# Block inverses of the gated-delta stage: even and odd columns in separate partitions, two masks dropped

## The chip, the core and the metric

The kernel runs on one core of one Trainium2 chip. The metric is the device time of one execution in microseconds (us); the table below gives the median of three runs.

## What is computed

One step of a hybrid decoder: a half-step SwiGLU feed-forward, a mixer, a second feed-forward, with 1,024 prompt tokens and 8 sequences of 8 new tokens. The mixer has two branches that are added under sigmoid gates: sliding-window attention (over the prompt, and of the new tokens over a cache of keys and values), and a gated delta rule with 8 heads of 128. The change is in the gated delta rule, in the inverse of a unit lower triangular matrix per head and chunk:

```python
    A = jnp.where(strict, jnp.einsum('bhnid,bhnjd->bhnij', kb, kc) * decay, 0.0)
    eye = jnp.eye(C, dtype=f32)
    T = lax.linalg.triangular_solve(A + eye, jnp.broadcast_to(eye, A.shape), left_side=True, lower=True)
    u_val = jnp.einsum('bhnij,bhnjv->bhniv', T, vb)
    w_key = jnp.einsum('bhnij,bhnjd->bhnid', T, kb * jnp.exp(gc)[..., None])
```

Outputs are the new token states, the last convolution rows, the recurrent matrices, keys and values.

## The kernel before

The work runs in one long program: first feed-forward, gates and prompt attention of the mixer, attention of the new tokens (`att_sample`, L974 to L1041, called sample attention below), the gated delta stage (`gdn`, L1224), the second feed-forward. A scheduler sets the order of each engine's queue; every engine then works its queue strictly in that order. Buffers come from pools that are stacked in one memory: when a stage ends, the next stage's pools are laid over the same addresses, and a tile may be written once every tile that held its addresses before has been read for the last time.

**Dense work.** For each head, q, k and v come from matmuls of the normed input with weight slices (L250 to L252, three passes, result `psgh` in three banks of PSUM). `conv_dense` copies them into a tile `ext` (pool "e", three buffers; L1178 clears its head, ACT copies at L1179, L1184 and L1186), `conv_taps` (L1200 to L1210) makes the convolution and SiLU from it, the tile `yh`. The dense matmuls are also what the program puts between the steps of slow chains, so that PE has work.

**Sample attention.** SP loads both caches (L983, L984). PE transposes the keys (L995, tile `pst`), makes scores (L1011, L1012, tile `pss`); a softmax on DVE and ACT; PE transposes the weights (L1026, L1027) into the tile `ptS`; then eight groups of sixteen matmuls (L1033, L1034) into the one bank `pso`, each copied out by DVE (L1039, eight copies). L1040 on DVE gates the sum and SP writes it out (L1041).

**The inverse** (`stage_t`, L1337). Per head k·kᵀ (L1351) gives nine chunks of 128x128, scaled to `am0` (L1367). They are written to memory (`adr`, L1377) and the 36 diagonal blocks of 32x32 are read back, one block to a partition (tile `L`, L1378). X starts as the identity (L1379, L1380). 31 steps of two DVE instructions (L1384 a product, L1385 a sum) make X the inverse of each block; step l works on (31−l) x (l+1) elements of each partition. L1389 makes the transposed copy, L1391 writes both to memory (`tdr`), L1397 loads them as diagonal blocks of 128x128 (`t4`, two groups of four chunks, each straight and transposed). `levels` (L1406) then joins blocks of 32 to 64 and of 64 to 128 with small matmuls (L1416, L1426, L1427, L1440, L1445); its weights are `am`, which POOL makes from `am0` by a mask multiplication (L1410, L1437). Then the chain over the chunks of the head (L1456 and on) uses the result.

`stage_t`, the chain and the gated output of a head run as generators beside the dense work (class `Weave`): each yields the PE time of its step and a gap, and dense steps are put in until the gap is over.

Of the kernel before, what the change touches and what calls it, by code (L numbers as in the profile page):

```python
# [9 lines left out]
F32 = mybir.dt.float32  # L10
# [3 lines left out]
ALU = mybir.AluOpType  # L14
# [4 lines left out]
P = 128  # L19
# [8 lines left out]
NCH = 9  # L28
# [4 lines left out]
BLK = 32  # L33
# [19 lines left out]
def constants():  # L53
# [17 lines left out]
        "m2": (j // 64 == i // 64) & (j % 64 < 32) & (i % 64 >= 32),  # L71
        "m3": (j < 64) & (i >= 64),
# [83 lines left out]
class Core:  # L156
# [1068 lines left out]
    def gdn(self):  # L1225
        nc, v = self.nc, self.nc.vector
        with ExitStack() as st:
            gp = self.pool("gdn", stack=st)
            a, n = self.off["m2"]
            self.m2 = gp.tile([P, 2, 32], F32, name="m2")  # L1230
            nc.sync.dma_start(self.m2, self.i["c_pack"][:, a:a + n].rearrange("p (b u j) -> p b u j", b=2, u=2)[:, :, 1, :])
            a, n = self.off["m3"]
            self.m3 = gp.tile([P, 64], F32, name="m3")
            nc.sync.dma_start(self.m3, self.i["c_pack"][:, a + 64:a + n])
# [12 lines left out]
            bp = Pools(self, st, ("L", "X", "pr", "am"), ("S0", "kg", "vt", "qk"), ("t4",), ("R", "o1", "vn", "S", "jk", "*"), ("ot", "zg", "me", "s4"), ("e",), ("y",), ("dm", "am0"))  # L1247
# [77 lines left out]

    def decay(self, bp, h, d):
# [11 lines left out]
    def stage_t(self, bp, h, d, prev):  # L1338
# [36 lines left out]
        L, X = (bp.tile([nb, BLK, BLK], F32, tag=x, bufs=1, name=self.name(x)) for x in ("L", "X"))  # L1375
        pr = bp.tile([nb, BLK * BLK // 4], F32, tag="pr", bufs=1, name=self.name("pr"))
        nc.sync.dma_start(self.rows_view(ad, 0), am0)  # L1377
        nc.gpsimd.dma_start(L, self.diag_view(ad, 0))  # L1378
        nc.gpsimd.memset(X, 0.0)  # L1379
        nc.gpsimd.memset(X.rearrange("p a b -> p (a b)")[:, ::BLK + 1], 1.0)  # L1380
        for l in range(BLK - 1):
            n, m = BLK - 1 - l, l + 1
            tmp = pr[:, :n * m].rearrange("p (a b) -> p a b", b=m)
            v.tensor_tensor(out=tmp, in0=L[:, l, m:, None].broadcast_to([nb, n, m]), in1=X[:, l, None, :m].broadcast_to([nb, n, m]), op=ALU.mult)  # L1384
            v.tensor_tensor(out=X[:, m:, :m], in0=X[:, m:, :m], in1=tmp, op=ALU.add)  # L1385
            if l % 2:
                yield 0, X_STEP
                self.lab = f"h{h}"
        v.tensor_copy(L, X.rearrange("p i j -> p j i"))  # L1389
        for u, src in enumerate((X, L)):  # L1390
            nc.gpsimd.dma_start(self.diag_view(td, u), src)  # L1391
# [14 lines left out]
    def levels(self, bp, h, A, t4):  # L1406
        nc, v = self.nc, self.nc.vector
        self.lab = f"h{h}"
        am = bp.tile([P, 4, 2, 32], F32, tag="am", bufs=2, name=self.name("am"))
# [532 lines left out]
```

## Time and profile before

| | us |
|---|---|
| median of three runs (2808.99 to 2811.06) | 2810.89 |
| the profiled execution | 2810.84 |
| span in its trace | 2809.1 |
| granted clock of TensorE, mean | 0.983 |
| PE busy | 2691.2 (96%) |
| DVE busy | 1982.4 (71%) |
| ACT busy | 1237.3 (44%) |
| POOL busy | 563.7 (20%) |

Times in the trace count from the start of the span. Of it, the sample attention and the gated delta stage take 1183 to 1957. The clock is the share of full speed that TensorE was granted; 1.00 is 2.4 GHz and 0.50 is 1.2 GHz. A time in brackets behind an instruction is the idle time of its engine just before it, with the instruction that ended it.

### The profile page before, as it was taken

How to read it: one execution, taken by the hardware profiler on the slowest of the kernel's cores; microseconds unless marked ns; L12 is line 12 of the kernel's file. 1: busy time of each engine (PE TensorE's matmuls, PEld its weight loads, DVE VectorE, ACT ScalarE, POOL GpSimd, SP SyncE). 2: the span in 40 equal slices, each digit the busy share in tenths (PEclk: the TensorE clock that was granted, in tenths of full speed). 3: DMA queues.
4: the chain of work that ended last, by engine and by line, in shares of the span. 5: the costliest groups of instructions: out<-in, count | busy, mean ns of one | idle time of the engine just before them, and what ended most of it. 6: DMA issues, size and time to landing. Idle time of an engine off the chain costs nothing.

```text
span 2809.1 us, 50868 instructions
## 1 busy us (share of the span) xinstructions
PE 2691.2 (96%) x19887; PEld 2523.4 (90%) x19887; DVE 1982.4 (71%) x4502; ACT 1237.3 (44%) x2904; POOL 563.7 (20%) x585
## 2 busy tenths in 40 slices
PE   6999999999989999999999999999999999998998
PEld 6899999999978888887788888888989999997998
DVE  6777787564665777777887776785678878767545
ACT  5333322233334767753655455546444233223333
POOL 3222221231010000031332222221002212205110
PEclk9999999999999999999999999999999999999999
DMA  4243322546332333342333333334533322216562
GB/s 143 91 158 127 112 101 90 191 135 144 107 105 54 85 85 78 97 100 63 90 98 78 67 94 90 89 82 145 191 118 117 103 88 102 100 57 237 129 147 78
DMA packets 236871, 306.66 MB, mean 109 GB/s; under 512 B 14405, under 2 KB 184214, under 8 KB 236598
## 3 DMA queue, kind: packets, MB, share of 16 engines
q1 hardware_dynamic: 203252, 222.21, 25.9%
q0 software_dynamic: 33312, 81.19, 10.6%
q8 instruction: 156, 2.56, 0.4%
q14 instruction: 85, 0.70, 0.1%
q10 hardware_dynamic: 66, 0.02, 0.0%
HBM read 212.19 MB, written 84.19 MB: 106 GB/s over the span
## 4 chain that ended last, share of the span: by engine, by line
PE 77%; DVE 9%; DMA 5%; ACT 3%; issue 3%; POOL 1%; SPq 0%; DVEq 0%; ACTq 0%; POOLq 0%
PE pst L252 13%; PE pst L250 13%; PE pst L251 13%; PE pst L715 4%; PE pst L714 4%; PE pst L713 4%; PE psgh L250 3%; PE psgh L251 3%; PE psgh L252 3%; PE psg L250 3%; PE psg L252 3%; PE psg L251 3%; PE pso L943 1%; DMA adr<-am0h 1%; PE pst L936 1%
## 5 line engine op out<-in xcount | busy, mean ns | idle before, releaser
L251 PE MATMUL pst<-x,u 128*128 128x256 f32 (+3 forms) x2656 | 780.4, 294 | 1.0 <-DVE x L226 1.0
L250 PE MATMUL pst<-x,u 128*128 128x256 f32 (+3 forms) x2040 | 610.8, 300 | 12.1 <-ACT x L225 11.1
L252 PE MATMUL pst<-x,u 128*128 128x256 f32 (+3 forms) x2040 | 605.6, 297 | 0.0
L251 PEld LDWEIGHTS pst<-x,u 128*128 128x128 f32 x2656 | 503.8, 190 | 7.1 <-DVE x L226 1.5
L250 PEld LDWEIGHTS pst<-x,u 128*128 128x128 f32 x2040 | 386.3, 190 | 19.3 <-ACT x L225 12.6
L252 PEld LDWEIGHTS pst<-x,u 128*128 128x128 f32 x2040 | 387.4, 190 | 4.6
L225 ACT CAST u<-raw 128x512 fp32r<-128x512 f32 x308 | 186.4, 617 | 323.3 <-PE pst L252 300.6
L715 PE MATMUL pst<-x,u 128*128 128x272 f32 x1008 | 293.3, 292 | 13.8 <-DVE u L226 13.8
L252 PE MATMUL psgh<-xhl,wlh 128*128 128x512 f32 (+2 forms) x912 | 303.7, 333 | 0.0
L713 PE MATMUL pst<-x,u 128*128 128x272 f32 x1008 | 290.6, 292 | 7.4 <-ACT x L225 7.1
L714 PE MATMUL pst<-x,u 128*128 128x272 f32 x1008 | 293.2, 292 | 4.5 <-DVE x L226 4.5
L226 DVE TENSOR_TENSOR u<-raw,u 128x512 fp32r<-128x512 f32 x308 | 216.5, 712 | 49.6 <-ACT u L225 49.3
L334 DVE TENSOR_TENSOR tm<-pst,tm 128x256 f32<-128x256 f32 (+1 forms) x400 | 168.0, 434 | 103.0 <-PE pst L252 100.9
L252 PE MATMUL pst<-xhl,u 128*128 128x256 f32 (+2 forms) x808 | 237.8, 295 | 2.5 <-DVE u L226 2.5
L250 PE MATMUL pst<-xhl,u 128*128 128x256 f32 (+2 forms) x808 | 236.7, 294 | 2.2 <-ACT u L225 2.2
L715 PEld LDWEIGHTS pst<-x,u 128*128 128x128 f32 x1008 | 192.8, 191 | 14.6 <-DVE u L226 14.6
L713 PEld LDWEIGHTS pst<-x,u 128*128 128x128 f32 x1008 | 191.6, 192 | 8.3 <-ACT x L225 7.5
L714 PEld LDWEIGHTS pst<-x,u 128*128 128x128 f32 x1008 | 192.9, 191 | 4.9 <-DVE x L226 4.9
L252 PEld LDWEIGHTS psgh<-xhl,wlh 128*128 128x128 f32 x912 | 172.9, 190 | 12.2
L252 PEld LDWEIGHTS pst<-xhl,u 128*128 128x128 f32 x808 | 153.2, 190 | 5.9 <-DVE u L226 2.9
L250 PEld LDWEIGHTS pst<-xhl,u 128*128 128x128 f32 x808 | 152.8, 190 | 5.3 <-ACT u L225 2.4
L250 PE MATMUL psg<-xhl,whc 128*128 128x512 f32 (+2 forms) x456 | 153.3, 336 | 1.1 <-DVE ring L814 1.1
(686 smaller groups left out, 6356.3 us busy)
## 6 DMA issues: line engine op xcount, KB each, us to landing
raw<-in_w_ffn_in_dram SPq DMA_DIRECT2D x48, 1024.0 KB
h<-hq SPq DMA_DIRECT2D x56, 544.0 KB
hq<-sg POOLq DMA_DIRECT2D x45, 544.0 KB, 3.6
rawh<-in_w_in_dram SPq DMA_DIRECT2D x38, 512.0 KB
w<-in_w_ffn_out_dram SPq DMA_DIRECT2D x14, 1024.0 KB
raw<-in_w_in_dram SPq DMA_DIRECT2D x21, 512.0 KB
ring<-ring SPq DMA_DIRECT2D x32, 272.0 KB
t4h<-tdr POOLq DMA_DIRECT2D x32, 256.0 KB, 5.1
```

The costliest lines, as they stand in the source:

```text
L225: keep(self.nc.scalar.copy(hi, src))
L226: return keep(self.nc.vector.tensor_tensor(out=lo, in0=src, in1=hi.bitcast(F32), op=ALU.subtract))
L250: nc.tensor.matmul(out, w[0], x[0], start=start, stop=False)
L251: nc.tensor.matmul(out, w[0], x[1], start=False, stop=False)
L252: nc.tensor.matmul(out, w[1], x[0], start=False, stop=stop)
L334: v.tensor_tensor(out=out, in0=pb, in1=t[:, i, :n], op=ALU.add)
L713: nc.tensor.matmul(pb, w[0], y[0], start=first, stop=False, skip_group_check=True)
L714: nc.tensor.matmul(pb, w[0], y[1], start=False, stop=False, skip_group_check=True)
L715: nc.tensor.matmul(pb, w[1], y[0], start=False, stop=end, skip_group_check=True)
L936: nc.tensor.transpose(out=pt[:, kb, r], in_=sm[:, r, kb * P:(kb + 1) * P], identity=self.ident)
L943: nc.tensor.matmul(po, w[:, ks // P + kb].rearrange("p a b -> p (a b)"), x[:, kb].rearrange("p r q -> p (r q)"), start=i + kb == 0, stop=i ...
```

## The change

Two partitions hold one block now: the first 36 the even columns of X, the next 36 the odd ones, sixteen columns each. So L is loaded twice, by two DMAs, X has half the elements to a partition, and step l of the 31 works on (31−l) x (l//2+1) elements. Over the 31 steps that is 2,856 elements to a partition for each of the two kinds of instruction, where it was 5,456. The diagonal of X is written by two copies of a small constant `half`. Each of the two writes to `tdr` becomes two, one for either half of the partitions: for X two with 1,152 runs of 64 bytes (before one with 1,152 of 128), for the transposed copy two with 576 runs of 128 bytes (before one with 1,152). X lies in memory with the even columns of a block ahead of the odd ones, and the matmuls and one copy of `levels` read and write it through permuted views. The weights of `levels` are slices of `am0` itself, without the mask: the rows that the mask would clear meet zeros of `t4`. The constants m2 and m3, their two loads and all 32 mask multiplications are gone.

The tiles of the stage get smaller: X has 2,048 bytes of each partition (before 4,096), `pr` 576 (1,024), `am` with its two buffers is gone (2,048), and so are m2 and m3 (512, for 32 with `half`): 5,024 bytes in all. What lies above them in the stack moves down by as much. The first `ext` tile lay at bytes 103,392 to 108,000 of a partition and lies at 98,368 to 102,976 now; the two `ptS` buffers of the sample attention lie at 97,408 to 99,456 in both programs. The lines of the changed kernel are those of before minus 1 from the table of constants to `gdn`.

```diff
--- before.py
+++ after.py
@@ -68,8 +68,7 @@
         "suf": j > i,
         "sufs": same8 & (j > i),
         "m1": (j // 32 == i // 32) & (j % 32 < 16) & (i % 32 >= 16),
-        "m2": (j // 64 == i // 64) & (j % 64 < 32) & (i % 64 >= 32),
-        "m3": (j < 64) & (i >= 64),
+        "half": np.arange(P)[:, None] // (NBK * NCH) == np.arange(2)[None, :],
         "bm": (np.arange(P)[:, None] // 8 == np.arange(NB)[None, :]),
         "band": np.where(band, 0.0, NEG),
         "first": np.where(first, 0.0, NEG),
@@ -1226,12 +1225,9 @@
         nc, v = self.nc, self.nc.vector
         with ExitStack() as st:
             gp = self.pool("gdn", stack=st)
-            a, n = self.off["m2"]
-            self.m2 = gp.tile([P, 2, 32], F32, name="m2")
-            nc.sync.dma_start(self.m2, self.i["c_pack"][:, a:a + n].rearrange("p (b u j) -> p b u j", b=2, u=2)[:, :, 1, :])
-            a, n = self.off["m3"]
-            self.m3 = gp.tile([P, 64], F32, name="m3")
-            nc.sync.dma_start(self.m3, self.i["c_pack"][:, a + 64:a + n])
+            a, n = self.off["half"]
+            self.half = gp.tile([P, 2], F32, name="half")
+            nc.sync.dma_start(self.half, self.i["c_pack"][:, a:a + n])
             self.gn = self.cols[:, 32:33]
             self.x2z = gp.tile([P, 4, 2, 32], F32, name="x2z")
             self.x3z = gp.tile([P, 4, 64], F32, name="x3z")
@@ -1244,7 +1240,7 @@
             for u in range(2):
                 for z in range(2):
                     nc.gpsimd.dma_start(self.rows_view(self.td[u], z), self.rsm[:, None, :].broadcast_to([P, NCH, P]))
-            bp = Pools(self, st, ("L", "X", "pr", "am"), ("S0", "kg", "vt", "qk"), ("t4",), ("R", "o1", "vn", "S", "jk", "*"), ("ot", "zg", "me", "s4"), ("e",), ("y",), ("dm", "am0"))
+            bp = Pools(self, st, ("L", "X", "pr"), ("S0", "kg", "vt", "qk"), ("t4",), ("R", "o1", "vn", "S", "jk", "*"), ("ot", "zg", "me", "s4"), ("e",), ("y",), ("dm", "am0"))
             hd = [dict() for _ in range(H)]
             wv = Weave(self)
 
@@ -1323,6 +1319,13 @@
     def diag_view(self, t, z):
         return bass.AP(t[:].tensor, t[:].offset + z * SCR, [[SCH, NBK * NCH], [SROW, BLK], [1, BLK]])
 
+    def half_view(self, t, z, p):
+
+        o = t[:].offset + z * SCR
+        if z == 0:
+            return bass.AP(t[:].tensor, o + p * (BLK // 2), [[SCH, NBK * NCH], [SROW, BLK], [1, BLK // 2]])
+        return bass.AP(t[:].tensor, o + p * SROW, [[SCH, NBK * NCH], [2 * SROW, BLK // 2], [1, BLK]])
+
     def decay(self, bp, h, d):
         self.lab = f"h{h}"
         nc = self.nc
@@ -1372,23 +1375,31 @@
             yield 0, 1.0
         self.lab = f"h{h}"
         nb = NBK * NCH
-        L, X = (bp.tile([nb, BLK, BLK], F32, tag=x, bufs=1, name=self.name(x)) for x in ("L", "X"))
-        pr = bp.tile([nb, BLK * BLK // 4], F32, tag="pr", bufs=1, name=self.name("pr"))
+        hw = BLK // 2
+        L = bp.tile([2 * nb, BLK, BLK], F32, tag="L", bufs=1, name=self.name("L"))
+        X = bp.tile([2 * nb, BLK, hw], F32, tag="X", bufs=1, name=self.name("X"))
+        pr = bp.tile([2 * nb, 144], F32, tag="pr", bufs=1, name=self.name("pr"))
         nc.sync.dma_start(self.rows_view(ad, 0), am0)
-        nc.gpsimd.dma_start(L, self.diag_view(ad, 0))
+        for p in range(2):
+            nc.gpsimd.dma_start(L[p * nb:(p + 1) * nb], self.diag_view(ad, 0))
         nc.gpsimd.memset(X, 0.0)
-        nc.gpsimd.memset(X.rearrange("p a b -> p (a b)")[:, ::BLK + 1], 1.0)
+        for p in range(2):
+            nc.gpsimd.tensor_copy(X.rearrange("p a b -> p (a b)")[:, p * hw::2 * hw + 1], self.half[:2 * nb, p:p + 1].broadcast_to([2 * nb, hw]))
         for l in range(BLK - 1):
-            n, m = BLK - 1 - l, l + 1
-            tmp = pr[:, :n * m].rearrange("p (a b) -> p a b", b=m)
-            v.tensor_tensor(out=tmp, in0=L[:, l, m:, None].broadcast_to([nb, n, m]), in1=X[:, l, None, :m].broadcast_to([nb, n, m]), op=ALU.mult)
-            v.tensor_tensor(out=X[:, m:, :m], in0=X[:, m:, :m], in1=tmp, op=ALU.add)
+            n, m, w = BLK - 1 - l, l + 1, l // 2 + 1
+            sh = [2 * nb, n, w]
+            tmp = pr[:, :n * w].rearrange("p (a b) -> p a b", b=w)
+            v.tensor_tensor(out=tmp, in0=L[:, l, m:, None].broadcast_to(sh), in1=X[:, l, None, :w].broadcast_to(sh), op=ALU.mult)
+            v.tensor_tensor(out=X[:, m:, :w], in0=X[:, m:, :w], in1=tmp, op=ALU.add)
             if l % 2:
                 yield 0, X_STEP
                 self.lab = f"h{h}"
-        v.tensor_copy(L, X.rearrange("p i j -> p j i"))
-        for u, src in enumerate((X, L)):
-            nc.gpsimd.dma_start(self.diag_view(td, u), src)
+        XT = L[:, :hw]
+        v.tensor_copy(XT, X.rearrange("p i j -> p j i"))
+        for p in range(2):
+            q = slice(p * nb, (p + 1) * nb)
+            nc.gpsimd.dma_start(self.half_view(td, 0, p), X[q])
+            nc.gpsimd.dma_start(self.half_view(td, 1, p), XT[q])
         d["X"] = True
         d["T"] = []
         for g in range(2):
@@ -1406,14 +1417,11 @@
     def levels(self, bp, h, A, t4):
         nc, v = self.nc, self.nc.vector
         self.lab = f"h{h}"
-        am = bp.tile([P, 4, 2, 32], F32, tag="am", bufs=2, name=self.name("am"))
-        nc.gpsimd.tensor_tensor(out=am, in0=A.rearrange("p c (b u j) -> p c b u j", b=2, u=2)[:, :, :, 1, :],
-                                in1=self.m2[:, None].broadcast_to([P, 4, 2, 32]), op=ALU.mult)
         px = self.bank("o").rearrange("p (w c b j) -> p w c b j", w=2, c=4, b=2)
         for c in range(4):
             for b in range(2):
                 lo, hi = b * 64, b * 64 + 32
-                nc.tensor.matmul(px[hi:hi + 32, 0, c, b], am[:, c, b], t4[:, c, 0, lo:hi], start=True, stop=True, tile_position=(0, hi))
+                nc.tensor.matmul(px[hi:hi + 32, 0, c, b], A[:, c, hi:hi + 32], t4[:, c, 0, lo:hi].rearrange("p (h j) -> p j h", h=2), start=True, stop=True, tile_position=(0, hi))
         yield .5, LHOP
         self.lab = f"h{h}"
         for b in range(2):
@@ -1429,15 +1437,13 @@
         self.lab = f"h{h}"
         for b in range(2):
             lo, hi = b * 64, b * 64 + 32
-            v.tensor_copy(t4[hi:hi + 32, :, 0, lo:hi], px[hi:hi + 32, 1, :, b])
+            v.tensor_copy(t4[hi:hi + 32, :, 0, lo:hi].rearrange("p c (h j) -> p c j h", h=2), px[hi:hi + 32, 1, :, b].rearrange("p c (j h) -> p c j h", h=2))
             nc.scalar.copy(t4[lo:hi, :, 1, hi:hi + 32], px[lo:hi, 1, :, b])
         yield 0, LHOP
         self.lab = f"h{h}"
-        am = bp.tile([P, 4, 64], F32, tag="am", bufs=2, name=self.name("am"))
-        nc.gpsimd.tensor_tensor(out=am, in0=A[:, :, 64:], in1=self.m3[:, None, :].broadcast_to([P, 4, 64]), op=ALU.mult)
         px = self.bank("o").rearrange("p (w c j) -> p w c j", w=2, c=4)
         for c in range(4):
-            nc.tensor.matmul(px[64:, 0, c], am[:, c], t4[:, c, 0, 0:64], start=True, stop=True, tile_position=(0, 64))
+            nc.tensor.matmul(px[64:, 0, c], A[:, c, 64:], t4[:, c, 0, 0:64].rearrange("p (b h j) -> p b j h", b=2, h=2), start=True, stop=True, tile_position=(0, 64))
         nc.scalar.copy(self.x3z[64:], px[64:, 0])
         yield .45, LHOP
         self.lab = f"h{h}"
```

**PE, behind the prompt attention.** L943 (now L942) is the last matmul of the prompt attention. Before, with the dense work of head 0's k behind it:

```order
7697 L943 MATMUL pso_12675<-th_12671,vl_11919 128x256 x2
7698 L943 MATMUL pso_12675<-tl_12672,vh_11918 128x256 x2
7699 L250 MATMUL psgh_1532_13271<-xhl_7668,whc_1520_13149 128x512
7700 L251 MATMUL psgh_1532_13271<-xhl_7668,whc_1520_13149 128x512
7701 L252 MATMUL psgh_1532_13271<-xhl_7668,wl_13150 128x512
7702 L250 MATMUL psgh_1532_13271<-xhl_7668,whc_1520_13149 128x512
```

In the changed program, where L994 is L995 of before, the transposes of the cached keys:

```order
7697 L942 MATMUL pso_12675<-th_12671,vl_11919 128x256 x2
7698 L942 MATMUL pso_12675<-tl_12672,vh_11918 128x256 x2
7699 L994 MATMUL pst_12705<-ident_60,kcache 128x128 x4
7700 L994 MATMUL pst_12711<-ident_60,kcache 128x128 x4
7701 L994 MATMUL pst_12717<-ident_60,kcache 128x128 x4
7702 L994 MATMUL pst_12723<-ident_60,kcache 128x128 x4
7703 L1010 MATMUL pss_12740<-kct,qs_s 32x128
7704 L1011 MATMUL pss_12740<-k_smp,qs_s 32x64
```

The dense work no longer stands here. It comes behind the last matmul of the sample attention (L1033, before L1034); between the two, at 7,699 to 7,846, there is none:

```order
7844 L1033 MATMUL pso_13072<-ptS_13070,vnd 128x128
7845 L1032 MATMUL pso_13072<-ptS_13070,vcd_13045 128x128
7846 L1033 MATMUL pso_13072<-ptS_13070,vnd 128x128
7847 L249 MATMUL psgh_1532_13269<-xhl_7668,whc_1520_13147 128x512
7848 L250 MATMUL psgh_1532_13269<-xhl_7668,whc_1520_13147 128x512
7849 L251 MATMUL psgh_1532_13269<-xhl_7668,wl_13148 128x512
```

**DVE, same place.** L948 (now L947) is its last instruction for the prompt attention. Before, the clearing of the first three `ext` tiles follows, and the first taps of the convolution; L996 comes behind these:

```order
1676 L948 SCALAR_TENSOR_TENSOR sgb_12315<-sgb_12315,pso_12675 64x128 x2
1677 L1178 MEMSET exth_1522_13153 128x3
1678 L1200 MEMSET yh_1526_13237 128x64
1679 L1178 MEMSET exth_1531_13268 128x3
1680 L1200 MEMSET yh_1548_13411 128x64
1681 L1178 MEMSET exth_1552_13428 128x3
1682 L1200 MEMSET yh_1559_13523 128x64
1683 L1200 MEMSET yh_1567_13636 128x64
1684 L1200 MEMSET yh_1589_13826 128x64
1685 L1208 SCALAR_TENSOR_TENSOR yh_1526_13237<-exth_1522_13153,cw,yh_1526_13237 128x1024
```

In the changed program the copies of the transposed keys (L995) follow:

```order
1676 L947 SCALAR_TENSOR_TENSOR sgb_12315<-sgb_12315,pso_12675 64x128 x2
1677 L1199 MEMSET yh_1526_13235 128x64
1678 L1199 MEMSET yh_1548_13409 128x64
1679 L1199 MEMSET yh_1559_13523 128x64
1680 L1199 MEMSET yh_1567_13636 128x64
1681 L1199 MEMSET yh_1589_13826 128x64
1682 L995 COPY kct<-pst_12705 128x512
```

and the `ext` tiles come behind L1039, which was L1040, the end of the sample attention:

```order
1765 L1038 COPY os<-pso_13028 64x2x8 x8
1766 L1038 COPY os<-pso_13072 64x2x8 x8
1767 L1039 SCALAR_TENSOR_TENSOR os<-sg_smp,os 128x512
1768 L1177 MEMSET exth_1522_13151 128x3
1769 L1177 MEMSET exth_1531_13266 128x3
1770 L1177 MEMSET exth_1552_13426 128x3
1771 L1207 SCALAR_TENSOR_TENSOR yh_1526_13235<-exth_1522_13151,cw,yh_1526_13235 128x1024
```

**PE, the first level of head 0.** L1416 of before is L1424 now; `t4h` is the loaded inverse. Before:

```order
8371 L252 MATMUL psgh_1677_14418<-xhl_7672,wlh_1599_13941 128x320
8372 L250 MATMUL psgh_1677_14418<-xhl_7672,whc128h_1598_13940 128x320
8373 L1416 MATMUL psoh_1611_14077<-t4h_1606_14049,amh_1610_14075 32x32 x8
8374 L251 MATMUL psgh_1677_14418<-xhl_7672,whc128h_1598_13940 128x320
8375 L252 MATMUL psgh_1677_14418<-xhl_7672,wlh_1599_13941 128x320
```

In the changed program:

```order
8292 L251 MATMUL psgh_1628_14229<-xhl_7668,wlh_1599_13941 128x512
8293 L249 MATMUL psgh_1628_14229<-xhl_7668,whc128h_1598_13940 128x512
8294 L1424 MATMUL psoh_1610_14079<-t4h_1606_14051,am0h_1536_13326 32x32 x8
8295 L250 MATMUL psgh_1628_14229<-xhl_7668,whc128h_1598_13940 128x512
8296 L251 MATMUL psgh_1628_14229<-xhl_7668,wlh_1599_13941 128x512
```

It stands 79 rows sooner, among dense work of an earlier weight slice: 66 dense matmuls fewer (and the transposes L1456 and L1457 of head 0's first chunks, and k·kᵀ of head 1 in part) lie before it. From head 2 on the place of every head's L1416 in PE's order is the same in both programs.

## Rows read from the trace of the kernel before

**Rows 1.** Windows view, length, then busy (count) of PE, PEld, DVE, ACT, POOL; clock, DMA.

```profile
1183.00:1957.00 774.00, 735.23 (x5618) 645.45 (x5617) 557.41 (x1764) 411.94 (x1211) 191.51 (x237) 0.98 0.36 92
1183.10:1236.00 52.90, 49.57 (x439) 43.23 (x438) 35.28 (x165) 30.48 (x76) 19.39 (x32) 1.00 0.41 119
```

**Rows 2.** Timeline of PE: start, length (us), instruction, [idle before it <-releaser].

```profile
1182.77 0.51 PE L943 MATMUL pso<-tl,vh 128*128 128x256 f32 x2
...
1193.89 1.16 PE L1351 MATMUL psgh<-yh 128*128 128x128 f32 x8 [1.70 <-ACT yh L1210]
...
1196.06 1.03 PE L995 MATMUL pst<-ident,kcache 128*128 128x128 f32 x8
...
1234.06 0.39 PE L1034 MATMUL pso<-ptS,vnd 128*128 128x128 f32 x2
```

**Rows 3.** Windows view, PE's work on psgh, pso, pst and pss, in that order.

```profile
1183.10:1236.00 52.90, 27.55 (x149) 1.00 0.41 119
1183.10:1236.00 52.90, 16.21 (x130) 1.00 0.41 119
1183.10:1236.00 52.90, 5.35 (x32) 1.00 0.41 119
1183.10:1236.00 52.90, 4.84 (x128) 1.00 0.41 119
```

**Rows 4.** Timeline of DVE, the last groups of the sample attention.

```profile
1230.80 1.47 DVE L1039 COPY os<-pso 64x16 f32<-64x16 f32 x8 [1.41 <-PE pso L1034]
1234.48 1.47 DVE L1039 COPY os<-pso 64x16 f32<-64x16 f32 x8 [2.21 <-PE pso L1034]
```

**Rows 5.** Timeline of SP, and the windows view while the caches are loaded.

```profile
1187.37 0.45 SPq L983 DMA_DIRECT2D kcache<-in_cache_swa_k_dram  x1
...
1192.00:1196.00 4.00, 2.30 (x18) 2.12 (x17) 0.00 (x0) 3.96 (x4) 0.00 (x0) 1.00 1.08 374
```

**Rows 6.** Windows view of PE before the stage: busy, granted clock, DMA.

```profile
776.00:780.00 4.00, 1.44 (x10) 1.00 0.34 105
...
788.00:792.00 4.00, 0.27 (x3) 0.89 0.00 0
792.00:796.00 4.00, 3.45 (x8) 0.50 0.45 131
796.00:800.00 4.00, 4.00 (x15) 0.76 0.00 0
```

**Rows 7.** Timeline of PE, first level matmuls of head 0.

```profile
1308.71 0.45 PE L1416 MATMUL psoh<-t4h,amh 128*32 128x32 f32 x16 [3.70 <-DMA t4h<-tdr]
```

**Rows 8.** Groups by form on DVE, 1180 to 1960: busy, mean ns, idle before.

```profile
L1389 DVE COPY Lh<-Xh 36x1024 f32<-36x1024 f32 x8 | 8.8, 1099 | 0.2
...
L1384 DVE TENSOR_TENSOR prh<-Lh,Xh 36x256 f32<-36x256 f32 x8 | 3.3, 414 | 0.2
...
L1384 DVE TENSOR_TENSOR prh<-Lh,Xh 36x31 f32<-36x31 f32 x16 | 3.0, 187 | 26.5 <-DMA Lh<-adr 26.2
```

**Rows 9.** Groups on POOL, same stretch.

```profile
L1437 POOL TENSOR_TENSOR amh<-am0h,m 128x256 f32<-128x256 f32 x16 | 12.3, 766 | 50.3 <-PE psoh L1440 50.3
...
L1391 POOL DMA_DIRECT2D tdr<-Xh x8 | 10.5, 1310 | 110.1 <-DVE Xh L1385 51.4 <-issue 37.6 <-DVE qkh L1462 12.5
```

**Rows 10.** DMA issues, same stretch: KB each, us to landing.

```profile
Lh<-adr POOLq DMA_DIRECT2D x8, 144.0 KB, 3.9
tdr<-Xh POOLq DMA_DIRECT2D x8, 144.0 KB, 6.3
tdr<-Lh POOLq DMA_DIRECT2D x8, 144.0 KB, 8.0
```

**Rows 11.** PE's waits, same stretch: us in total, times, longest.

```profile
PE psoh L1416 <- DMA t4h<-tdr: 4.9, 2, 3.7
PE psth L1456 <- DVE qkh L1462: 4.7, 4, 1.7
PE psth L1456 <- DVE zgh L1646: 4.0, 2, 2.5
```

## The prediction

> **What bounds the kernel.** I read the windows view of the stage first. Over the 774 us from 1183 to 1957 PE is busy 735.2, DVE 557.4, POOL 191.5 [rows 1]. So PE is the bound, with 38.8 us idle, and its clock is 0.98, which is worth some 15 us more (0.02 x 774, an estimate). DVE, whose work the change halves in places, is idle 28% of the time. A saving on DVE or POOL counts only where PE waits for it. The list of PE's waits says how much that is: for the loaded inverse `t4h` 4.9 us, for DVE's `qkh` and `zgh` 4.7 and 4.0 [rows 11]. I then laid PE's timeline at the start of the stage beside the order of both programs, because that is where they differ most.
>
> **Part 1: the smaller X.** Product rows of 31 and of 256 elements take 187 and 414 ns [rows 8]: 1.01 ns an element and some 156 ns fixed. 2,600 elements fewer for each kind make 2 x 2.6 = 5.2 us a head, the copy of half the 1,024 elements (1,099 ns) about 0.5: DVE is 5.7 us shorter a head, 46 us over eight. POOL loses 32 masks (16 of them 12.3 us, 766 ns each [rows 9]), about 24 us.
>
> **Part 2: the transfers.** A write of X costs POOL 1.31 us to issue [rows 9] and lands in 6.3 us, that of the copy in 8.0; the load of L lands in 3.9 [rows 10]. The second load of L goes out one issue later, +1.3 us at most. Of the four writes the last is issued two issues later, +2.6. There are 3,456 runs in place of 2,304. If a run costs the same whatever its length, the last landing is up to 4 us later (half of 8.0); if bytes count, nothing. So the inverse comes 5.7 − 1.3 − 2.6 = 1.8 us sooner at best and 2.2 later at worst, about as late as before. From head 2 on PE meets it in the same order, and in eight heads it has waited for it twice in all [rows 11]. I cost this at nothing; what covers it is the dense work ahead of L1416, and without that cover it would cost the 2.2 us at each head.
>
> **Part 3: the memory that moves.** Here is the main term. The first `ext` tile now ends above byte 98,368 and so shares 64 bytes with one `ptS` buffer and 1,024 with the other. It may be cleared only when the last group of the sample attention has read them. Before, it lay above both. In the order, DVE's three clearings, ACT's copies out of `psgh` and with them PE's dense work stand behind the sample attention, where they stood before or within it. How long does PE lose? It ended the prompt attention at 1182.77 + 0.51, and the first transposes of the cached keys began at 1196.06 [rows 2]. The load of the keys is issued at 1187.37 and the DMA engines are still full at 374 GB/s in 1192 to 1196 [rows 5], so the keys can't be used sooner: PE stands still from 1183.3 to about 1195. After that the groups go through the one bank `pso` in turn. The last two copies, which waited for PE, are 3.68 us apart [rows 4], and by then little else was on DVE. Without dense work the groups keep that pace: the chain through one bank doesn't speed up. So the sample attention ends near 1234 as before, and what PE did meanwhile on `psgh` comes afterwards. That work is 27.55 us between 1183.1 and 1236 [rows 3], of which up to 1.8 lies behind the last L1034 at 1234.06 [rows 2]: 25.8 at most. At least it is what the other three tiles leave of PE's 49.57 busy us [rows 1, 3]: 49.57 − 16.21 − 5.35 − 4.84 = 23.2, less 1.8, 21.4 (overlapping matmuls are counted in both, hence the two ends). I take 22.5, nearer the low end, since one k·kᵀ may find its input sooner than the 1.70 us that PE waited [rows 2].
>
> **Part 4: the clock in that stretch.** Before this stage PE had a stretch with 0.27 us of work in 4 us, after which the clock was 0.50 for four us and 0.76 for four more; but after one with 1.44 us of 4 it was still 1.00 [rows 6]. In the changed kernel PE stands still for nearly 12 us and then has 16.21 us of `pso` work in eight groups of 3.68, about 55% busy. At full clock through the groups this adds nothing; at half clock throughout, the 16.21 us of matmuls, which lie on the chain, double: +16.2. The rows show half clock for some 6 us after a pause, and nothing of how groups with pauses between them go on. I take 7, a little under the middle.
> The Trainium skill, "TensorE: Matmul & The Clock Gate", Part 1, says that the throttled state is the default and that activity releases it. By that rule the caches' wait is sure to end at half clock, as [rows 6] show, and groups with pauses in them may stay there: the term would be 16.2 and the sum 9 us higher.
>
> **Part 5: the first two heads.** L1416 of head 0 waited 3.70 us for its inverse, to 1308.71 [rows 7], of 4.9 in all [rows 11]. It stands 66 dense matmuls sooner now; at 27.55/149 = 0.185 us each [rows 3] that is 12 us of PE's work. PE would reach it at 1305.0 + 22.5 − 12 = 1315. The inverse follows from a k·kᵀ that comes at 1234 + 10.8 = 1245 now (10.8 is from the first dense matmul to L1351 [rows 2]), sooner ahead of L1416 than in the old order but with DVE free of the sample attention. I can't time that chain from the trace. If both waits vanish it gives 5 us back; if each of the two heads waits as long as that 4.9, it costs 5 more. I take 0.
>
> **Part 6: what DVE and POOL give back.** Later in the stage PE waits 8.7 us for `qkh` and `zgh` [rows 11], both made by DVE between steps of X, and part of the 15 us of lost clock follows such pauses. All of it would be −24, none of it 0. I take −8: DVE is 8% lighter (46 of 557), and shorter X steps shorten just these queues, but other chains stay.
>
> **Sum.** 22.5 + 7 + 0 − 8 = +21.5 us on the profiled execution of 2810.84, which is the median of the runs within 0.1 us: **2832.3**. Its ends, all terms at one side: 21.4 − 5 − 24 = −8, and 25.8 + 16.2 + 5 = +47; as not all of them will go one way, about +6 to +37.
>
> **Rivals.**
> *The relief wins (faster).* One mechanism: X is what holds up DVE's queue, and with it 5.7 us shorter a head PE's waits and the clock behind them go in all heads from 1 on. For it: PE idles 38.8 us in the stage [rows 1], and the masks go as well. Against it: only 8.7 us of waits name DVE here, and the start costs 21.4 even at full clock. It would need −24 and the 5 of `t4h`, and some more; all 38.8 gone would give 2810.8 + 21.4 − 38.8 = 2793. It decides if PE's idle time behind the sample attention falls by over 27 us. I give 0.08.
> *The lag is given back (same).* The displaced dense work later fills pauses that PE had: 21.4 lost, 24 returned by Part 6, near 2808. Against it: from head 2 on the order is the same, so no dense work gets into old pauses. 0.10.
> *Half clock through the sample attention (slower still).* 22.5 + 16.2 + 0 − 4, and the scores and transposes too (5.35 + 4.84 us [rows 3], of which I count half): 2850. This is what the rule of the clock gate named above would make. 0.15.
> *The change doesn't do what it says: the inverse comes no sooner but later.* The runs of 64 bytes land as slowly as those of 128, and every head waits 2.2 us more, with 3 us of half clock at some: 8 x 2.2 + 22.5 + 7 gives 2858. Against it: the two waits of 4.9 us in eight heads show slack at the others. 0.07.
> Beside this stands a rule of the Trainium skill, "DMA: Bandwidth & Descriptors", Specifications: transfers below 512 bytes don't reach line rate. Both sizes here are below; no row of before separates 64 from 128.
>
> **The numbers.** The forecast (2832, from 2817 to 2848) has 0.60. A time within 0.2% (5.6 us) of 2810.9 can't be told from no change by this measurement. Faster has the first rival, 0.08; same the second, 0.10; slower the rest, 0.82. The range leaves out the first rival and the far parts of the others: 2812 to 2855.
>
> **What would show it.** Right: in the changed trace PE is idle from 1183 to about 1195 and waits for DVE's copies between the groups; the last `os` copy ends near 1236 to 1243; the first dense matmul of head 0's k follows it; the granted clock is at 0.5 for part of 1190 to 1235; k·kᵀ of head 0 moves from 1193.9 to about 1245; the end of the stage comes some 20 us later, and DVE is busy some 46 us less. Wrong: the sample attention ends ten us sooner than 1234, because its groups were held up by other work on DVE and ACT and can run faster alone; then the start costs only 12. Or PE's idle time in 1250 to 1957 falls by more than 20 us.

## The result

The changed kernel takes 2854.0 us (median of four runs, 2850.6 to 2858.6), the kernel before 2809.9: a ratio of 1.016, 95% interval 1.0144 to 1.0176, 44 us slower. The direction was forecast, the size was not: +21.5 us was. The time lies above the 2817 to 2848 of the forecast and 1 us below the top of its wider range, 2812 to 2855. The profiled execution took 2856.1.

The page's first part: PE has as many instructions as before, DVE is busy 50 us less (1982.4 before), POOL 10 us less (563.7).

```profile
PE 2701.9 (95%) x19887; PEld 2533.1 (89%) x19887; DVE 1932.3 (68%) x4502; ACT 1233.2 (43%) x2900; POOL 553.3 (19%) x585
```

The stage itself, now 1181 to 2001, in the windows view; the row answers to the first of [rows 1]. It is 46 us longer, PE busy 747 us in it, DVE 509 in place of 557, and the clock is 0.96.

```profile
1181.00:2001.00 820.00, 746.95 (x5611) 656.03 (x5610) 508.92 (x1758) 405.98 (x1204) 180.22 (x237) 0.96 0.35 87
```

PE's timeline at the start, shortened; L942, L994, L1032, L249 and L1354 are L943, L995, L1033, L250 and L1351 of [rows 2]. PE waits 10.8 us for the cached keys and does no dense work until the eight groups are over. k·kᵀ of head 0 comes 44 us later than before.

```profile
1180.62 0.50 PE L942 MATMUL pso<-tl,vh 128*128 128x256 f32 x2
1191.94 3.64 PE L994 MATMUL pst<-ident,kcache 128*128 128x128 f32 x16 [10.82 <-DMA kcache<-in_cache_swa_k_dram]
...
1199.95 0.46 PE L1032 MATMUL pso<-ptS,vcd 128*128 128x128 f32 x2 [0.55 <-ACT ptS L1028]
...
1227.63 0.39 PE L1033 MATMUL pso<-ptS,vnd 128*128 128x128 f32 x2
1228.89 0.50 PE L249 MATMUL psgh<-xhl,whc 128*128 128x512 f32 x1 [0.88 <-ACT exth L1183]
...
1237.87 2.22 PE L1354 MATMUL psgh<-yh 128*128 128x128 f32 x18
```

The clock there (length, PE busy, clock, DMA share, GB/s) falls to 0.50 while PE stands still and is 1.00 from 1196 on, through the groups. The last two rows below are the busiest and the least busy windows of the groups, 84% and 59%.

```profile
1184.00:1188.00 4.00, 0.00 (x0) 0.50 0.98 352
...
1192.00:1196.00 4.00, 4.00 (x37) 0.60 0.49 166
...
1200.00:1204.00 4.00, 3.37 (x39) 1.00 0.00 0
...
1224.00:1228.00 4.00, 2.34 (x20) 1.00 0.98 235
```

PE's waits in the stage (us in total, times, longest). The two made by DVE, 8.7 us in [rows 11], are down to 2.2 for `qkh` and 0.3 for `zgh`. In the first place stands a wait that was small before: POOL's product `kgmh` (L1574 before, L1580 now), with which the sample states of each head are updated; PE reads it at L1583.

```profile
PE psth L1583 <- POOL kgmh L1580: 22.6, 6, 5.2
PE pst L994 <- DMA kcache<-in_cache_swa_k_dram: 10.8, 1, 10.8
PE psoh L1424 <- DMA t4h<-tdr: 8.7, 2, 6.2
PE pso L1032 <- DVE os L1038: 7.7, 7, 1.7
...
PE psth L1462 <- DVE qkh L1468: 2.2, 4, 0.7
```

The same wait in the kernel before:

```profile
PE psth L1577 <- POOL kgmh L1574: 2.7, 4, 1.4
```

There are two such products to a head, with one buffer, so POOL may make the second only when PE has read the first. POOL's timeline around the second product of head 5 shows that it stands behind the four writes of an inverse and the four loads of t4. The first of these loads holds POOL for 6.96 us, until the second write of X has landed. PE had finished with the first product at 1827.1. In POOL's order the second product stands so in six of the eight heads, 0 and 2 to 6.

```profile
1810.46 1.03 POOL L1580 TENSOR_TENSOR kgmh<-kgh,bm 128x512 f32<-128x512 f32 x1 [6.42 <-DMA sdh<-soh]
1818.14 1.06 POOL L1401 DMA_DIRECT2D tdr<-Xh  x1 [6.64 <-DVE Xh L1393]
1819.19 0.79 POOL L1402 DMA_DIRECT2D tdr<-Lh  x1
1819.97 0.97 POOL L1401 DMA_DIRECT2D tdr<-Xh  x1
1820.93 0.76 POOL L1402 DMA_DIRECT2D tdr<-Lh  x1
1828.65 3.02 POOL L1408 DMA_DIRECT2D t4h<-tdr  x4 [6.96 <-DMA tdr<-Xh]
1831.68 1.05 POOL L1580 TENSOR_TENSOR kgmh<-kgh,bm 128x512 f32<-128x512 f32 x1
```

In the kernel before (head 2) the same product stands between the loads, and from head 3 on ahead of the first load:

```profile
1507.50 1.60 POOL L1391 DMA_DIRECT2D tdr<-Xh  x1 [12.53 <-DVE qkh L1462]
1509.10 0.99 POOL L1391 DMA_DIRECT2D tdr<-Lh  x1
1514.42 0.78 POOL L1397 DMA_DIRECT2D t4h<-tdr  x1 [4.33 <-DMA tdr<-Xh]
1515.22 1.05 POOL L1574 TENSOR_TENSOR kgmh<-kgh,bm 128x512 f32<-128x512 f32 x1
```

What follows on PE in the changed kernel, for head 5, is a pause of 4.38 us and then a lower clock:

```profile
1828.00:1832.00 4.00, 0.41 (x3) 1.00 0.59 167
1832.00:1836.00 4.00, 3.21 (x14) 0.69 0.65 177
```

### The profile page after: what moved, and what is told of

It reads as the page before. It is cut to its first block, busy times and chain, and to the rows that moved or that the text cites. A ratio compares the mean times of both kernels' runs of the same rounds, so it can differ in the third digit from the quotient of the medians.

```text
span 2854.3 us, 50888 instructions
## 1 busy us (share of the span) xinstructions
PE 2701.9 (95%) x19887; PEld 2533.1 (89%) x19887; DVE 1932.3 (68%) x4502; ACT 1233.2 (43%) x2900; POOL 553.3 (19%) x585
## 4 chain that ended last, share of the span: by engine, by line
PE 75%; DVE 8%; DMA 7%; issue 4%; ACT 2%; POOL 2%; SPq 0%; DVEq 0%; POOLq 0%; ACTq 0%
PE pst L251 13%; PE pst L249 13%; PE pst L250 13%; PE pst L714 4%; PE pst L713 4%; PE pst L712 4%; PE psgh L249 3%; PE psg L249 3%; PE psg L251 2%; PE psg L250 2%; PE psgh L250 2%; PE psgh L251 2%; DMA tdr<-Xh 2%; PE pso L942 1%; DMA Lh<-adr 1%
## 5 line engine op out<-in xcount | busy, mean ns | idle before, releaser
L250 PE MATMUL pst<-x,u 128*128 128x256 f32 (+3 forms) x2656 | 778.9, 294 | 1.3 <-DVE x L225 1.3
L249 PE MATMUL pst<-x,u 128*128 128x256 f32 (+3 forms) x2040 | 609.0, 299 | 12.1 <-ACT x L224 11.1
L250 PEld LDWEIGHTS pst<-x,u 128*128 128x128 f32 x2656 | 502.3, 189 | 7.2 <-DVE x L225 1.8
L249 PEld LDWEIGHTS pst<-x,u 128*128 128x128 f32 x2040 | 384.7, 189 | 19.0 <-ACT x L224 12.5
L714 PE MATMUL pst<-x,u 128*128 128x272 f32 x1008 | 294.6, 293 | 13.5 <-DVE u L225 13.5
L249 PE MATMUL pst<-xhl,u 128*128 128x256 f32 (+2 forms) x808 | 236.8, 295 | 2.2 <-ACT u L224 2.2
L249 PEld LDWEIGHTS pst<-xhl,u 128*128 128x128 f32 x808 | 152.7, 190 | 5.3 <-ACT u L224 2.4
L249 PE MATMUL psg<-xhl,whc 128*128 128x512 f32 (+2 forms) x456 | 153.3, 336 | 1.1 <-DVE ring L813 1.1
```

What stands on the lines that cost most here:

```text
L249: nc.tensor.matmul(out, w[0], x[0], start=start, stop=False)
L250: nc.tensor.matmul(out, w[0], x[1], start=False, stop=False)
L714: nc.tensor.matmul(pb, w[1], y[0], start=False, stop=end, skip_group_check=True)
```

## The experiments

Ratios are to runs of the kernel before on the same chip; in brackets stands the 95% interval. 0.001 is 2.8 us. The runs were made on several chips, on which the kernel before itself takes 2808 to 2818 us, so traces of different runs are compared to within some microseconds only.

**The moved memory alone.** In the kernel before, X and its products go behind `ext` in the stack of pools; nothing else changes.

```diff
-("L", "X", "pr", "am"), ... ("e",), ("y",)
+("L", "am"), ... ("e",), ("X", "pr"), ("y",)
```

> The kernel before, nothing changed but the place of X and its products in the stack of pools: behind ext and not below it, so that ext lies 5,120 bytes lower and overlaps the two ptS buffers, as in the change. Theory A: some 28 us slower than before, 2838 us, with PE idle from 1183 to about 1192 and no dense work until the sample attention is over. Theory B (what the start loses comes back later, in pauses that the kernel before has): 2810 to 2820 us.

1.0058 (1.0043 to 1.0073), 16 us slower (12 to 21): Theory A in kind, though its 28 us are too many. PE's timeline shows the same start as in the change:

```profile
1194.01 3.87 PE L995 MATMUL pst<-ident,kcache 128*128 128x128 f32 x16 [12.38 <-DMA kcache<-in_cache_swa_k_dram]
...
1233.17 0.50 PE L250 MATMUL psgh<-xhl,whc 128*128 128x512 f32 x1 [0.88 <-ACT exth L1184]
```

So the overlap of `ext` with the two `ptS` buffers moves the dense work behind the sample attention, and the moved memory costs 16 us, less than the 22.5 of the forecast. The sample attention hardly ends sooner in this trace: from the last L943 to the last L1034 it is 50.8 us, 51.3 before. One of its groups ran at a lower clock:

```profile
1204.00:1208.00 4.00, 3.27 (x33) 0.75 0.00 0
```

Why 16 and not 22.5 is not shown by this run.

**The change with ext in its old place.** A first try put an unused tile into the stage's first pool and cleared it on POOL.

> The change with an unused tile of 5,024 bytes in the stage's first pool, so that the ext tiles lie where they lay before; in the order the clearings of ext and the dense work stand ahead of the sample attention again. Theory A (the displaced start costs some 28 us, what is behind it some 16 us comes from POOL's second kgm product, which stands behind the loads of t4): 2854 - 28 = 2826 us, the first dense matmul back near 1183, kk of head 2 near 1359, PE's wait for kgm still 20 us or more. Theory B (the start costs little, since dense work only moves; the loss is the inverse's slower transfers): 2845 to 2854 us. Theory C (the relief of DVE is worth more than the kgm wait costs, only the start hid it): under 2810 us.

1.0138 (1.0123 to 1.0154), near the time of Theory B. But the tile's clearing waited 9 us for L1039 and held up what stands behind it on POOL, the zeroing of `tdr` too (1237.6 in place of 1222.1): the run says little. With the tile in a pool of its own below `ext`, never written:

```diff
-("ot", "zg", "me", "s4"), ("e",)
+("ot", "zg", "me", "s4"), ("pad",), ("e",)
```

> The change with an unused, never written tile of 5,024 bytes in a pool of its own just below ext (in the first try the tile's clearing on POOL waited for the end of the sample attention and held up the zeroing of tdr behind it, 1237 in place of 1229 us). If the moved memory costs within the change what it cost the kernel before (ratio 1.0058, some 16 us): ratio about 1.010, and kk of head 2 near 1365. If the losses cover each other (with the dense work ahead of it, PE waits for the inverse of the first two heads instead): 1.013 or more, L1416's wait for t4 over 12 us.

1.0114 (1.0099 to 1.013): the memory costs 0.0046 within the change, some 13 us. Both of the expectation's signs appear, the ratio near 1.010 and PE's longer wait for the first heads' inverse:

```profile
PE psth L1584 <- POOL kgmh L1581: 26.6, 7, 5.6
PE psoh L1425 <- DMA t4h<-tdr: 16.7, 2, 8.4
```

**The product kgm.** On DVE in place of POOL (`nc.gpsimd` to `nc.vector` in its line), in the change, with the first and with the second tile (e1's and e8's), and in the kernel before:

> The change with the kgm products on DVE in place of POOL; memory as in the change. Theory A: PE's wait for kgm (22.6 us in the change) and the half clock behind it go, some us of DVE's time come back as waits: 2854 - 20 = 2834 us, kk of head 2 still near 1387. Theory B (the wait for kgm hides another wait on the same chain, the inverse of the next head or the sample states): 2850 us or more, with the wait at another instruction of the same place.

> Both of the last two: the unused tile and kgm on DVE. Theory A: the two losses are separate and add up: 2854 - 28 - 20 = 2806 us, a little below the kernel before, by the relief of DVE. If one wait covers the other: 2815 to 2825 us. If the change is a loss by itself (two halves, four writes): over 2815 us with PE waiting for t4.

> The same tile below ext, and kgm on DVE. Additive losses: ratio 1.0048 - 0.0058 = 0.999. Covered losses: 1.002, as the first try of the pair gave. If only the zeroing of tdr was in the way there: 0.997 or less.

> The kernel before with kgm on DVE, as a control: there PE waited 2.7 us for kgm, so ratio 0.998 to 1.002. If moving kgm is a gain by itself, apart from the order that the change made on POOL: 0.995 or less.

1.0048 (1.0031 to 1.0065) for the change; 1.0019 (1.0010 to 1.0028) with the first tile; 1.0003 (0.9993 to 1.0013) with the second; 1.0038 (1.0023 to 1.0053) for the kernel before. So this move costs the kernel before 11 us, more than was expected of the control, and gives the change 31, with either place of `ext` (1.016 to 1.0048, 1.0114 to 1.0003): nothing that the wait hid takes its place. With two buffers for its tag (which also serves two other tiles, `to` and `so`) both products stand ahead of the writes in POOL's order:

```diff
-kgm = bp.tile([P, 4, P], F32, tag="s4", bufs=1, ...)
+kgm = bp.tile([P, 4, P], F32, tag="s4", bufs=2, ...)
```

> The change with two buffers in place of one for the tag s4, which holds kgm: the second product need not wait until PE has read the first, and in POOL's order both stand ahead of the four writes of the inverse; the 2,048 bytes more also lift ext above the ptS buffers, so that the dense work stands within the sample attention again. If the wait behind the loads of t4 is the main loss (theory A) and the memory the other: both go, ratio 0.996 to 1.002, PE's wait for kgm under 3 us. If kgm on DVE had helped by something else (POOL free for the loads): 1.005 or more.

> Two buffers for kgm, and an unused tile of 2,976 bytes below ext, so that ext lies just where it lay in the kernel before. If the two losses are all that the change loses: under 1.000, since kgm no longer costs DVE time as in the runs before, 0.995 to 0.999, 2797 to 2807 us where the kernel before takes 2810. If the wait of the first two heads for the inverse (14 to 17 us in all three repaired kernels, 4.9 before) is a third loss of the change that outweighs DVE's relief: 1.000 to 1.004.

Without a tile, 1.0062 (1.0047 to 1.0077), in the range of the second case, but with a cause of its own, which the trace shows in part: `ext` lies clear of `ptS`, but at another place than before, and ACT has work of head 0's decay, which waits 5.05 us for its load, ahead of the copies to `ext`; PE waits 6.3 us for these. With the tile, 0.9999 (0.9990 to 1.0008). PE's waits there:

```profile
PE psoh L1425 <- DMA t4h<-tdr: 18.2, 2, 9.3
PE pssh L1503 <- DVE Sh L1524: 6.5, 7, 1.2
```

None for kgm is left. From 1.0114 to 0.9999 are 32 us: this is the price of the second kgm product in the wrong place. The wait for t4 is 18.2 us, where the kernel before has 4.9: the third loss that the expectation speaks of is there.

**Which part turns the order round.** The masks left out of the kernel before, and the split with the masks kept, both with `ext` in its old place:

> The kernel before with the masks of the levels left out and nothing else; an unused tile keeps ext in its place. POOL has 24 us less work, PE waited once 1.8 us for it: 0.998 to 1.001. If the masks were what kept the second kgm product ahead of the loads of t4, the wait for kgm appears here: 1.008 or more.

> The change with the masks kept (m2, m3 and am as before, and the mask products); an unused tile keeps ext in its place. If the split alone turns POOL's order round: the loss of the change without its moved memory, 1.009 to 1.013, with PE's wait for kgm over 20 us. If it takes both parts: under 1.004.

The masks alone: 0.9983 (0.9974 to 0.9993), faster by 5 us. The split alone: 1.012 (1.0103 to 1.0136), with the wait of the change:

```profile
PE psth L1597 <- POOL kgmh L1594: 27.9, 7, 6.6
```

So the split turns the order round, and the masks have no part in it. Then two halves of the split, both without the masks. A short X (w columns for m in the 31 steps, 36 partitions, two writes), with one buffer for kgm and with two. These two kernels leave out the columns of X from l//2+1 on, so they don't compute the inverse; they serve for their time alone:

```diff
-n, m = BLK - 1 - l, l + 1
+n, m, w = BLK - 1 - l, l + 1, l // 2 + 1
```

> The kernel before without the masks, ext in its place, in which each of the 31 steps works on l//2+1 columns in place of l+1; 36 partitions, one load, two writes as before. It leaves out the columns of X from l//2+1 on. In POOL's order the second kgm product of heads 3 to 7 stands behind the loads of t4, as in the change. If the shorter X alone makes the loss: PE's wait for kgm 15 us or more and a ratio of 1.004 to 1.010. If the four writes in a row are needed for it to cost: under 1.001.

> As e16 with two buffers for kgm, so that both products stand ahead of the writes; the same columns of X are left out. No split, no long wait for kgm: it shows what the shorter X is worth. If the split's transfers are what takes the gain of e10 back: 0.990 to 0.995. If a shorter X is worth little, because DVE is not the bound: 0.997 to 0.999, as the masks alone.

1.0015 (1.0006 to 1.0023) and 1.0009 (1.0001 to 1.0018); neither meets one of the values expected. In the first the order of POOL is turned round in heads 2 to 6 with two writes as before, so the shorter X is enough to do it; presumably the scheduler has the writes and loads ready sooner and puts them first. But the price is small, 8.2 us of waits for kgm:

```profile
PE psth L1567 <- POOL kgmh L1564: 8.2, 6, 2.2
```

```profile
1601.54 1.42 POOL L1386 DMA_DIRECT2D tdr<-Xh  x1 [6.71 <-DVE Xh L1380]
1602.95 1.01 POOL L1386 DMA_DIRECT2D tdr<-Lh  x1
1607.94 1.54 POOL L1392 DMA_DIRECT2D t4h<-tdr  x2 [3.98 <-DMA tdr<-Xh]
...
1611.24 1.49 POOL L1392 DMA_DIRECT2D t4h<-tdr  x2 [0.80 <-DMA tdr<-Lh]
...
1613.35 1.05 POOL L1564 TENSOR_TENSOR kgmh<-kgh,bm 128x512 f32<-128x512 f32 x1
```

From the first write to the product pass 11.8 us here, 13.5 in the change, and POOL's wait at the first load is 3.98 us, against 6.96. And four writes with a long X, each of the old writes cut into two of 18 partitions:

> The kernel before without the masks, ext in its place, with each of the two writes of the inverse sent as two, by 18 partitions each: four writes, but 2,304 runs of 128 bytes as before. If the number of writes makes the inverse late: from the end of X to the last load of t4 16 us or more (11.3 to 12.3 before, 15 to 18 in the change), ratio 1.001 to 1.004. If the number of runs does it: under 13.5 us and 0.998 to 1.000.

0.9985 (0.9976 to 0.9994), as the masks alone: four writes in place of two cost nothing. The DMA issues (number, KB each, median us to landing) for the masks alone, for four writes, and for the change:

```profile
tdr<-Xh POOLq DMA_DIRECT2D x8, 144.0 KB, 7.0
tdr<-Lh POOLq DMA_DIRECT2D x8, 144.0 KB, 9.4
```

```profile
tdr<-Xh POOLq DMA_DIRECT2D x16, 72.0 KB, 4.2
tdr<-Lh POOLq DMA_DIRECT2D x16, 72.0 KB, 5.9
```

```profile
tdr<-Xh POOLq DMA_DIRECT2D x16, 72.0 KB, 7.3
tdr<-Lh POOLq DMA_DIRECT2D x16, 72.0 KB, 7.6
```

A write of X has 1,152 runs of 128 bytes in the first, 576 of 128 in the second, 1,152 of 64 in the third. The medians, 7.0, 4.2 and 7.3 us, mislead for the change, where the second write of X goes out third, behind a write of the copy. Two of them one by one, issued at 1914.19 and 1916.02:

```profile
tdr<-Xh POOLq DMA_DIRECT2D x1, 72.0 KB, 5.5
tdr<-Xh POOLq DMA_DIRECT2D x1, 72.0 KB, 9.0
```

Read so, the eight first writes of X in the change land in 5.2 to 7.1 us, the eight that go out third in 7.4 to 9.5. The eight of the masks alone take 6.5 to 7.4, the eight first ones of the four-write run 3.3 to 5.3. So half the bytes in as many runs save some 1 us of 7 (medians 5.9 and 7.0), half the bytes in half the runs 3 (median 3.8). The writes of the four-write run also come from half the partitions, so whether runs or partitions count is not shown.

POOL's first load needs both writes of X. In the change they have landed 9.2 to 11.3 us after the first was issued, with the masks alone 6.5 to 7.4: POOL is held longer because the second half of X waits its turn. Sending both halves of X ahead of the two copies, as the four-write run does, was not tried in the change.

**Versions.** The masks left out with two buffers for kgm, and e10 with the second half's writes on SP's queue:

> The kernel before without the masks and with two buffers for kgm, ext in its place. PE waits 3.7 us for kgm in the run with the masks alone (0.9983): 0.995 to 0.998 if that wait goes and the clock with it. If the earlier kgm products get in the way of others on POOL or PE, as DVE's copy of S in e10: 0.999 to 1.001.

> As e10, and the two writes of the second half of the partitions go out on SP's queue, beside those of the first half on POOL's. If the four writes in a row on POOL are what makes the inverse late at the first two heads: the wait for t4 falls by 3 us or more and the time to 0.003 below that of e10. If the landing of the short runs is what takes long, or if the writes wait in SP's queue: the same as e10 or slower.

0.9995 (0.9986 to 1.0003) and 1.0022 (1.0013 to 1.0031): neither is better, and the wait for t4 stays, 18.7 us in e13. So two buffers by themselves gain nothing. The masks alone, `ext` in its place, are some 5 us (0.2%) faster than the kernel before, and nothing tried is clearly better.

**Where gains and losses lie.** The traces can be cut into three stretches at marks that every run has. Between them PE does the same work (its dense matmuls agree to within 3), so the lengths in us can be set beside each other. The marks are the last matmul of the prompt attention, k·kᵀ of head 1, k·kᵀ of head 3, and the last matmul that reads kgm. One trace stands for each run.

| | to k·kᵀ of head 1 | to k·kᵀ of head 3 | to the last kgm |
|---|---|---|---|
| the kernel before | 76.8 | 185.0 | 496.0 |
| the change | 96.9 | 196.7 | 513.1 |
| e8, `ext` in its old place | 76.8 | 200.2 | 516.8 |
| e10, two buffers as well | 77.5 | 201.0 | 484.5 |
| e11, the masks alone | 79.5 | 187.4 | 495.8 |
| e14, the masks and two buffers | 76.6 | 183.1 | 494.4 |
| e17, the same with a short X | 76.6 | 195.0 | 482.5 |

Runs e10 and e11 are from one chip; their second and third stretch in the windows view of PE, e10 first:

```profile
1258.66:1459.66 201.00, 172.72 (x1271) 0.91 0.38 78
1459.66:1944.16 484.50, 473.38 (x3662) 0.99 0.36 86
```

```profile
1260.04:1447.44 187.40, 174.72 (x1269) 0.94 0.33 76
1447.44:1943.24 495.80, 478.42 (x3677) 0.98 0.36 85
```

In the third stretch e10 is 11.3 us shorter than e11: DVE's relief is real. In the second it is 13.6 us longer, and there PE waits 18.2 us for t4, 5.0 in e11. e17 against e14, also from one chip, shows the same pair, 11.9 us shorter and 11.9 longer. From e8 to e10 all of the 32 us of kgm come off the third stretch.

## Why the prediction was right or wrong

- **Part 2, the step that failed.** "I cost this at nothing; what covers it is the dense work ahead of L1416". I looked for who waits for the inverse, and did not read what stands behind its loads in POOL's queue. The second kgm product stands there in six of eight heads, POOL is held for the landing, PE for POOL: 32 us, the largest term of all, shown by e8 against e10 (two buffers) and e8 against e9 (kgm on DVE). It could be read from POOL's order before any run, and was not among the rivals. The rival that came near the time (2858) had a late inverse at every head; PE waited for t4 in two. The transfers themselves came out within the bounds of Part 2: from the first write to the last load's issue POOL takes 12.8 to 17.3 us, 10.5 to 12.3 before, so they take back 1 to 6 us a head of the 5.7 that X gained. Part 2 doesn't have it that POOL's first load now waits for the write that goes out third and no longer for the first.
- **Part 1, right for DVE.** 46 us were forecast, 50 measured. POOL lost 10 us and not 24: the masks went, but the further writes and the second load of L are POOL's work too (28.4 us of writes for 18.4, 16.0 of loads for 8.3).
- **Part 3, right in its mechanism.** (The first `ext` tile begins at byte 98,368, where the text says that it ends above it; the overlap is as stated.) 22.5 us were forecast. The first stretch of the change is 20.1 us longer than before, and as before in e8. Of these 13 are left at the end (1.016 against 1.0114): against e8 the change wins back 3.5 and 3.7 us in the other two stretches, where PE waits less for t4 (8.7 us in all, 16.7 in e8). So a third of the lag is given back, as a rival had it for the whole. e5, in the kernel before, measured 16. The sample attention was shorter by some 4 us in the change: from the start of the last L942 to that of the last L1033 it is 47.0 us now (1227.63 less 1180.62); before, to the last L1034, 51.3 [rows 2]. "Without dense work the groups keep that pace" holds (3.68 us), but they began sooner. In e5 the whole is hardly shorter, 50.8.
- **Part 4, wrong.** 7 us were forecast, and in this trace none were lost in the groups. The lower clock covers the wait and the transposes of the keys, 3.64 us for the sixteen. The Trainium skill, "TensorE: Matmul & The Clock Gate", Part 1, says that the throttled state is the default and that activity releases it; the 0.50 of 1184 to 1192 and the 1.00 from 1196 on agree. What the prediction drew from it, that groups with pauses may stay at half clock, did not come about in the change; in e5 one group ran partly at half clock (0.82 and 0.75 in 1200 to 1208).
- **Part 5, wrong.** 0 was forecast. The second stretch is 11.7 us longer than before, 15 to 16 where the dense work stands early (e8, e10). The wait for t4 rose from 4.9 to 8.7 us, and to 14.5 to 18.7 with the dense work early. The late inverse is not all of it: e17 has no split, waits 9.0 us for t4 and still loses 11.9 us there to e14. Why is open.
- **Part 6, about right in size.** −8 was forecast; the third stretch gives back some 11 to 12 us (e10 against e11, e17 against e14). In the change itself the wait for kgm covers it, and over the whole stage the second stretch takes it back, so that neither e10 nor e17 is faster than its counterpart.

Together: 13 us for the memory and 32 for kgm make 45, where 44 were measured. This is no check of the two, since they are steps on one path from the change to e10, and e10 takes as long as the kernel before. What it says is that the rest cancels: DVE's relief from head 3 on against the loss at the first heads. The direction was right by the start; that the time still lies within 2812 to 2855 is luck, since its largest term was not in the sum.

## What to carry to other kernels

Where a change makes a step shorter, read the order of every queue that this step feeds, and ask what now stands behind its loads: here a load that waited 6.96 us for a write held a product of 1.05 us behind it on POOL, and PE with it. A smaller tile moves every tile above it; check which old tile each one now overlaps before counting the saving. Cut the traces at marks that all runs share before calling a saving worth nothing: 50 us off DVE, which was idle 28% of the time, gave some 11 us in the later heads, and the first heads lost as much.

## What the runs showed of the hardware

Writes from POOL with short runs, with nothing of the same inverse ahead of them: 1,152 runs of 128 bytes from 36 partitions landed in 6.5 to 7.4 us (masks alone), 1,152 of 64 bytes from 36 in 5.2 to 7.1 (the change), 576 of 128 bytes from 18 in 3.3 to 5.3 (four writes). Halving each run saved little, halving their number with the partitions saved more. "DMA: Bandwidth & Descriptors" (the Trainium skill, Specifications) puts the least transfer for line rate at 512 bytes; every run of bytes in these writes is shorter, so no trace here shows the other side. A write that went out third, within 2 us of the first, landed in 7.4 to 9.5 us.

TensorE's clock was 1.00 through 28 us of groups with pauses of up to 1.7 us between them (1200 to 1228), some 8 us after a pause of 10.8 us at 0.50. In e5 it was still 0.75 in one window of the groups.
